# A hybrid attention layer: shift and scale rows of the second modulation summed on TensorE instead of VectorE

## The chip, the cores and the metric

The kernel runs on one core of a Trainium2 chip. A core has five engines that run side by side, each through its own list of instructions in order: TensorE (PE; its weight loads are shown apart as PEld), VectorE (DVE), ScalarE (ACT), GpSimd (POOL) and SyncE (SP), which here only starts transfers (DMAs). Matrix products go from the on-chip memory SBUF into the accumulator memory PSUM, from where DVE or ACT read them. The metric is the time of one execution on the device, in microseconds (us).

## What is computed

One layer of a streaming encoder on 1024 positions of width 1024, in float32. Cut to what the change concerns:

```python
mod = jnp.dot(jax.nn.silu(c), w_ada[l]) + b_ada[l]          # c: (1, 1024), w_ada: (1024, 6144)
sh_a, sc_a, g_a, sh_m, sc_m, g_m = jnp.split(mod, N_MOD, axis=-1)
h = modulate(rmsnorm(x, g_attn_norm[l]), sh_a, sc_a)        # h * (1 + scale) + shift
...
x = x + g_a[:, None, :] * mixed                             # attention groups, output projection
h = modulate(rmsnorm(x, g_mlp_norm[l]), sh_m, sc_m)
u = causal_dwconv(jnp.dot(h, w_up[l]), conv_w[l], conv_b[l])
gate, val = jnp.split(u, 2, axis=-1)
x = x + g_m[:, None, :] * jnp.dot(jax.nn.silu(gate) * val, w_down[l])
```

The six rows of `mod` are numbered 0 to 5. Row 2 is the gate of the mixer, row 3 the shift and row 4 the scale of the second modulation, the one ahead of the MLP. Each is a product of a vector of 1024 numbers with a 1024 x 1024 block of weights, which is 4 MB to read for one row of output.

## The kernel before

The kernel keeps nearly float32 accuracy in its large products by splitting operands into a high and a low part and adding three products (lines 154 to 156, one after another for each pair of tiles). It goes through these phases: the first modulation and the first query/key projection; attention, together with the remaining projections; the output projection; the MLP.

In the attention phase two kinds of work are woven together. *Units* are attention heads over four query tiles (`Unit.scores` makes scores on PE at L758, minimum on DVE at L775 to L783, exponential on ACT at L790, the two halves of the probabilities on POOL and DVE at L73 and L812, and their transposition by DMA at L824; `Unit.values`, three tiles behind, multiplies by the values on PE at L852 and writes through L861 and L862). *Fillers* are generators that do projections in small portions: v0, qk1, qk2, v1 (tiles `ipv`), qk3 (`ipq`), m (the latent projection, tiles `mp`), then up0, up1 and oca. After each part of a unit, `pace` runs as many portions of fillers as its own cost in PE time calls for. `gemm3_f` lets a portion follow the unit work of `LAG` steps ago (the list `trail`).

A third generator, `f_ada`, is the one that is changed. It computes rows 2, 3 and 4 on the side: `fill_step` calls it once for each 1700 ns of filler cost in the fillers qk1 to m. `steps` lists 48 blocks of weights: for each row m, each half n of 512 columns, each of the eight k of 128 input positions. A block is 128 partitions x 512 float32, 256 KB, loaded by SP (L409) into one of the five buffers with tag "A". Three blocks are loaded ahead. For each block DVE multiplies it by the column `cs[:, k]` of silu(c), which is one number to a partition, and adds it to an accumulator `aacc` of 128 x 512 (L421 for the first block, L423 for the rest). After eight blocks the accumulator still has to be summed over its 128 partitions. For row 2 `gate_bcast` does it with a product by a matrix of ones, which leaves the sum on all partitions. For rows 3 and 4 four products of PE, with 128 columns of the accumulator as the stationary operand and one column of ones as the moving one (L436), give the 512 sums as four columns of 128, in a PSUM buffer of tag "mm"; ACT copies them to `modT` (L437). `modT` rows 3 and 2 then get the bias, the 1 and the gain (L440 to L442), and are first read in the MLP's modulation.

The "mm" buffers are two; the projections of the fillers use them in turn.

The order of instructions on each engine isn't written out by hand: the units' parts have priorities, `issue_after` keeps an instruction behind another one, and a scheduler, which works with a model of the engines' times, places the rest. Each engine then takes its list strictly in that order.

Of the kernel before, what the change touches and what calls it, by code (L numbers as in the profile page):

```python
# [13 lines left out]
F32 = mybir.dt.float32  # L14
# [4 lines left out]
AF = mybir.ActivationFunctionType  # L19
# [3 lines left out]
MUL, ADD, SUB, MIN, MAX = ALU.mult, ALU.add, ALU.subtract, ALU.min, ALU.max  # L23

P = 128
D = 1024
S = 1024
NT = S // P
ND = D // P
# [9 lines left out]
GSTEP, LAG = 2, 4  # L39
# [25 lines left out]
def layer_kernel(ctx, tc, I, out):  # L65
    nc = tc.nc
    pe, act, dve, pool, sp = nc.tensor, nc.scalar, nc.vector, nc.gpsimd, nc.sync
# [22 lines left out]
    ga_d = dram.tile([P, D], F32, name="ga_d")  # L90
# [9 lines left out]
    ones = cst.tile([P, P], F32, name="ones")  # L100
# [3 lines left out]
    modT = cst.tile([P, 4, ND], F32, name="modT")  # L104
    cs = cst.tile([P, ND], F32, name="cs")
# [26 lines left out]
    ps = psA.__enter__()  # L132
# [6 lines left out]
    def qtile(name):  # L139
        return apg.tile([P, 512], F32, name=name, tag="sq", bufs=2)  # L140

    def atile(name):
        return apg.tile([P, 512], F32, name=name, tag="A", bufs=5)
# [17 lines left out]
    trail = []  # L161
# [115 lines left out]
    for d in range(ND):  # L277
# [7 lines left out]
        pt = ps.tile([P, 512], F32, name=f"p_ada{d}", tag="mm", bufs=2)  # L285
# [14 lines left out]
        for t in range(NT):  # L300
            h, j = divmod(t, 4)
# [97 lines left out]
    def f_ada():  # L399
        steps = [(m, n, k) for m in (2, 3, 4) for n in range(2) for k in range(ND)]  # L400
        wt = {}

        def load(i):
            if i < len(steps):
                m, n, k = steps[i]
                wt[i] = atile(f"aw{m}_{n}_{k}")
                c0 = m * D + n * 512
                with tc.issue_after(anchor["sp"]):
                    sp.dma_start(wt[i][:], I["w_ada"][k * P:(k + 1) * P, c0:c0 + 512])  # L409

        for i in range(3):
            load(i)
        yield 0
        yield 0
        for i, (m, n, k) in enumerate(steps):
            if k == 0:
                acc = atile(f"aacc{m}_{n}")
            load(i + 3)
            with tc.issue_after(anchor["dve"]):
                if k == 0:  # L420
                    dve.tensor_scalar(acc[:], wt[i][:], cs[:, 0:1], None, op0=MUL)  # L421
                else:
                    dve.scalar_tensor_tensor(acc[:], wt[i][:], cs[:, k:k + 1], acc[:], op0=MUL, op1=ADD)  # L423
            yield 0
            if k < ND - 1:
                continue
            yield 0
            pt = ps.tile([P, 512], F32, name=f"p_ada{m}_{n}", tag="mm", bufs=2)
            if m == 2:
                gate_bcast(pt[:], acc, m * D + n * 512, 512, qtile)  # L430
                g = qtile(f"gab{n}")
                act.activation(g[:], pt[:], AF.Copy)
                sp.dma_start(ga_d[:, n * 512:(n + 1) * 512], g[:])
            else:
                for j in range(4):
                    pe.matmul(pt[:, j:j + 1], acc[:, j * P:(j + 1) * P], ones[:, 0:1], start=True, stop=True)  # L436
                act.activation(modT[:, 3 if m == 3 else 2, 4 * n:4 * n + 4], pt[:, 0:4], AF.Copy)  # L437
            yield 0
        b = pk[:, C_B + 24:C_B + 40].rearrange("p (a b) -> p a b", a=2)
        dve.tensor_tensor(modT[:, 3, :], modT[:, 3, :], b[:, 0], op=ADD)  # L440
        dve.tensor_tensor(modT[:, 2, :], modT[:, 2, :], b[:, 1], op=ADD)
        dve.scalar_tensor_tensor(modT[:, 2, :], modT[:, 2, :], 1.0, pk[:, C_GM:C_GM + ND], op0=ADD, op1=MUL)  # L442

    def gate_bcast(pt, acc, c0, w, alloc):

        br = alloc(f"brow{c0}")
        sp.dma_start(br[0:1, :w], I["b_ada"][:, c0:c0 + w])
        dve.tensor_tensor(acc[0:1, :w], acc[0:1, :w], br[0:1, :w], op=ADD)
        pe.matmul(pt, ones[:], acc[:, :w], start=True, stop=True)
# [458 lines left out]
    def mla_unit(gr, hh, g):  # L908
        o = hh % 2

        def prep():
# [13 lines left out]
               ("m", f_m()), ("up0", f_up(0)), ("up1", f_up(1)), ("oca", f_oca())]  # L925
    done = set()
    side = [f_ada()]
    nside = [0]

# [47 lines left out]
    for n in range(len(tiles) + DEPTH):  # L977
        if n < len(tiles):
            u, i = tiles[n]
# [4 lines left out]
        if n >= DEPTH:  # L984
            u, i = tiles[n - DEPTH]
# [131 lines left out]
    for t in range(NT):  # L1117
        pt = ps2.tile([P, 1024], F32, name=f"op{t}", tag="op", bufs=3)
# [371 lines left out]
    for t in range(4):  # L1490
        o = dl.tile([P, 512], F32, name=f"oe{t}", tag="oe", bufs=3)
# [78 lines left out]
```

## Time and profile before

| | |
|---|---|
| median of 3 runs | 1380.44 us (1379.88 to 1385.12) |
| the profiled execution: time | 1379.88 us |
| the profiled execution: span, first to last instruction | 1378.1 us |
| mean granted TensorE clock | 0.94 |
| transfers of the 48 blocks `aw` | started between 114.1 and 325.5 us |
| rows 3 and 4: products at L436 | between 246.0 and 336.0 us |

The profile is of one execution. Busy times are of each engine alone, so they overlap. The end of a matmul is modelled, so that matmuls that follow each other closely show as a PE that is always busy; the distance between their starts is then the better measure. The granted clock (PEclk) is the share of full speed at which PE was let run. In the lists of waits, a row names the instruction that waited, what it waited for, the total in us, how many times, and the longest. In rows of a time line, the columns are the start in us, the length in us, engine, line, operation, what is written and read, and how many were merged into the row.

### The profile page before, as it was taken

To read this page: it belongs to the slowest core of one execution; us is meant where nothing else is said; L and a number is where in the kernel's file an instruction comes from. 1 tells how busy PE (TensorE), PEld (TensorE's weight loads), DVE (VectorE), ACT (ScalarE), POOL (GpSimd) and SP (SyncE) were. 2 spreads that over 40 slices of the span, in tenths; PEclk is the share of its full clock that TensorE was granted. 3 is DMA by queue.
4 is the path that set the end of the run, shared out by engine and by line. 5 is a ranking of instruction groups with operands and counts; after the bars stand their busy time and mean duration, and the time that the engine had idled before them with its cause. 6 is when DMAs were issued, how large, how long until landed. Compare 5 with 4: busy or idle time off the path is not lost.

```text
span 1378.1 us, 18696 instructions
## 1 busy us (share of the span) xinstructions
PE 1229.5 (89%) x6168; PEld 1009.3 (73%) x6168; DVE 1105.8 (80%) x1928; ACT 622.0 (45%) x1131; POOL 572.2 (42%) x610
## 2 busy tenths in 40 slices
PE   4889698989867779886997999999999999999998
PEld 3788487977655567674775888777788888888886
DVE  6957878676589997885689689898988888688667
ACT  4443445444455554554365443434444444443341
POOL 5454556365646574343643443434444442200000
PEclk9999797999787989997998999999999999999999
DMA  8314557666322468678921233333323224983451
GB/s 321 129 41 91 135 144 189 157 137 146 64 50 74 81 141 183 136 136 204 376 101 46 87 128 104 121 128 116 109 92 113 92 100 142 340 308 119 130 161 61
DMA packets 223689, 190.57 MB, mean 138 GB/s; under 512 B 148708, under 2 KB 166884, under 8 KB 223592
## 3 DMA queue, kind: packets, MB, share of 16 engines
q1 hardware_dynamic: 223592, 189.38, 47.5%
q8 instruction: 48, 0.79, 0.2%
q14 instruction: 49, 0.40, 0.1%
HBM read 117.24 MB, written 37.49 MB: 112 GB/s over the span
## 4 chain that ended last, share of the span: by engine, by line
PE 44%; DVE 16%; issue 5%; ACT 4%; DMA 4%; POOL 2%; SPq 0%; ACTq 0%; DVEq 0%; POOLq 0%
PE p L1068 6%; PE p L1070 6%; PE p L1069 6%; PE dnA_P L1381 2%; PE dnA_P L1383 2%; PE dnA_P L1382 2%; PE sm L764 2%; DVE u L1235 2%; PE dnB_P L1383 1%; PE dnB_P L1381 1%; PE dnB_P L1382 1%; DMA adaw<-w_ada 1%; DVE hlm L812 1%; DVE u L1234 1%; PE pvm L852 1%
## 5 line engine op out<-in xcount | busy, mean ns | idle before, releaser
L77 ACT ACTIVATE dnP<-dnr 128x1024 fp32r<-128x1024 f32 x73 | 77.4, 1062 | 113.1 <-PE dnA_P L1383 46.4
L1355 DVE TENSOR_TENSOR dnP<-dnr,dnP 128x1024 fp32r<-128x1024 f32 x72 | 89.5, 1246 | 46.5 <-ACT dnP L77 46.5
L73 POOL TENSOR_SCALAR hlm<-Pm,rim 128x512 f16<-128x512 f32 (+3 forms) x96 | 66.6, 702 | 75.8 <-ACT Pm L790 21.2
L1234 DVE SCALAR_TENSOR_TENSOR u<-c,cvp,u 128x1023 f32<-128x1023 f32 x44 | 62.0, 1449 | 29.6 <-ACT u L1233 29.6
L84 POOL TENSOR_TENSOR wf<-wu,wf 128x512 fp32r<-128x512 f32 x22 | 35.8, 1628 | 118.5 <-ACT wf L77 118.5
L73 POOL TENSOR_SCALAR hlc<-Pc,ric 128x640 f16<-128x640 f32 (+2 forms) x64 | 47.4, 744 | 72.2 <-DVE ric L793 40.6
L812 DVE SCALAR_TENSOR_TENSOR hlm<-Pm,rim,hlm 128x512 f16<-128x512 f32 (+3 forms) x96 | 67.7, 714 | 8.8 <-POOL hlm L73 8.4
L790 ACT ACTIVATE Pm<-sm,mm 128x128 f32<-128x128 f32 (+3 forms) x64 | 47.2, 738 | 52.5 <-DVE mm L783 31.8
L84 POOL TENSOR_TENSOR wb<-wu,wb 128x512 fp32r<-128x512 f32 x22 | 38.8, 1763 | 73.1 <-ACT wb L77 72.1
L1233 ACT ACTIVATE u<-c,cvp 128x1024 f32<-128x1024 f32 x44 | 52.3, 1237 | 34.4 <-DVE c L1304 25.8
L1235 DVE SCALAR_TENSOR_TENSOR u<-c,cvp,u 128x1022 f32<-128x1022 f32 x44 | 64.8, 1512 | 0.0
L852 PE MATMUL pvm<-PTm,vt 128*128 128x256 f16 (+1 forms) x320 | 45.9, 295 | 20.9 <-DMA PTm<-hlm 13.9
L790 ACT ACTIVATE Pc<-sc,mc 128x640 f32<-128x640 f32 (+2 forms) x64 | 42.0, 657 | 48.5 <-DVE mc L779 35.8
L812 DVE SCALAR_TENSOR_TENSOR hlc<-Pc,ric,hlc 128x640 f16<-128x640 f32 (+2 forms) x64 | 53.5, 840 | 12.7 <-POOL hlc L73 12.5
L852 PEld LDWEIGHTS <-vt 128*128 128x128 f16 x320 | 31.9, 109 | 35.7 <-DMA PTm<-hlm 14.4
L154 PE MATMUL ipq<-wq_s,hT 128*128 128x256 f32 x192 | 55.9, 294 | 1.2 <-ACT wq_s L77 1.2
L155 PE MATMUL ipq<-wq_s,hT 128*128 128x256 f32 x192 | 56.4, 294 | 0.1
L156 PE MATMUL ipq<-wq_s,hT 128*128 128x256 f32 x192 | 56.0, 292 | 0.0
L77 ACT ACTIVATE wc<-ws 128x512 fp32r<-128x512 f32 x21 | 13.3, 632 | 93.6 <-DVE ws L1087 93.6
L1382 PE MATMUL dnA_P<-dnP 128*128 128x512 f32 x132 | 51.3, 389 | 0.0
L1383 PE MATMUL dnA_P<-dnP 128*128 128x512 f32 x132 | 51.3, 389 | 0.0
L1381 PE MATMUL dnA_P<-dnP 128*128 128x512 f32 x132 | 51.2, 389 | 0.0
(432 smaller groups left out, 4453.4 us busy)
## 6 DMA issues: line engine op xcount, KB each, us to landing
wu<-w_up SPq DMA_DIRECT2D x44, 512.0 KB, 3.8
dnr<-g_d SPq DMA_DIRECT2D x73, 256.0 KB, 4.4
aw<-w_ada SPq DMA_DIRECT2D x48, 256.0 KB, 3.5
g_d<-u SPq DMA_DIRECT2D x22, 512.0 KB, 2.8
dnr<-w_down SPq DMA_DIRECT2D x44, 256.0 KB, 5.6
adaw<-w_ada_a SPq DMA_DIRECT2D x16, 512.0 KB, 6.1
x<-x SPq DMA_DIRECT2D x16, 512.0 KB, 9.0
g_d<-gs SPq DMA_DIRECT2D x22, 256.0 KB, 2.2
```

Source lines behind the costliest of these rows:

```text
L73: pool.tensor_scalar(o, i, s, 1.0, op0=MUL, op1=MUL)
L77: act.activation(o, i, AF.Copy)
L790: act.activation(pr[:, :n], sv, AF.Exp, bias=m[:], scale=-1.0, accum_out=rsum[:, 0:1])
L812: dve.scalar_tensor_tensor(hl[:, w:2 * w], pp, ri[:], hl[:, :w], op0=MUL, op1=SUB)
L852: last = pe.matmul(dst, u.vst(j), mov, start=(x == 0), stop=(x == len(todo) - 1), skip_group_check=True)
L1068: pe.matmul(pt, sh, pg[:, 0], start=(k == 0 and not add), stop=False, skip_group_check=skip)
L1069: pe.matmul(pt, sh, pg[:, 1], start=False, stop=False, skip_group_check=skip)
L1235: dve.scalar_tensor_tensor(u[:, 2:], c[:, :S - 2], cvp[:, cv:cv + 1], u[:, 2:], op0=MUL, op1=ADD)
L1355: r = f(*a, **k)
L1381: pe.matmul(pt, sh, w[:, 0, 0], start=start, stop=False, skip_group_check=add)
L1382: pe.matmul(pt, sh, w[:, 1, 0], start=False, stop=False, skip_group_check=add)
L1383: pe.matmul(pt, sl, w[:, 0, 0], start=False, stop=stop, skip_group_check=add)
```

## The change

Row 2 stays as it was. For rows 3 and 4, DVE no longer accumulates. Instead PE takes the weight blocks themselves as stationary operands, 128 x 128 at a time, with the column `cs[:, k]` as the moving operand, and sums over four blocks in PSUM: `burst` makes four products (q) for each of four column groups (j), 16 in all. Two bursts make one half of a row: ACT copies the first result to `modT`, DVE adds the second to it. There are eight bursts. The loads of these 32 blocks still go one to a step of the generator, through the same five buffers; a burst uses four of them, and is called five steps after its first block's load. The steps of row 2 no longer start loads for row 3. The generator takes 34 steps for rows 3 and 4 instead of 40.

```diff
+        def burst(i):
+            m, n, k0 = steps[i]
+            pt = ps.tile([P, 512], F32, name=f"p_ada{m}_{n}_{k0}", tag="mm", bufs=2)
+            for j in range(4):
+                for q in range(4):
+                    pe.matmul(pt[:, j:j + 1], wt[i + q][:, j * P:(j + 1) * P], cs[:, k0 + q:k0 + q + 1],
+                              start=(q == 0), stop=(q == 3))
+            o = modT[:, 3 if m == 3 else 2, 4 * n:4 * n + 4]
+            if k0:
+                dve.tensor_tensor(o, o, pt[:, 0:4], op=ADD)
+            else:
+                act.activation(o, pt[:, 0:4], AF.Copy)
+
...
-        for i, (m, n, k) in enumerate(steps):
+        nrow = 2 * ND
+        for i, (m, n, k) in enumerate(steps[:nrow]):
             if k == 0:
                 acc = atile(f"aacc{m}_{n}")
-            load(i + 3)
+            if i + 3 < nrow:
+                load(i + 3)
...
-            if m == 2:
-                gate_bcast(pt[:], acc, m * D + n * 512, 512, qtile)
-                g = qtile(f"gab{n}")
-                act.activation(g[:], pt[:], AF.Copy)
-                sp.dma_start(ga_d[:, n * 512:(n + 1) * 512], g[:])
-            else:
-                for j in range(4):
-                    pe.matmul(pt[:, j:j + 1], acc[:, j * P:(j + 1) * P], ones[:, 0:1], start=True, stop=True)
-                act.activation(modT[:, 3 if m == 3 else 2, 4 * n:4 * n + 4], pt[:, 0:4], AF.Copy)
+            gate_bcast(pt[:], acc, m * D + n * 512, 512, qtile)
+            g = qtile(f"gab{n}")
+            act.activation(g[:], pt[:], AF.Copy)
+            sp.dma_start(ga_d[:, n * 512:(n + 1) * 512], g[:])
+            yield 0
+        for i in range(nrow, len(steps) + 2):
+            if i % 4 == 1 and i > nrow + 1:
+                with tc.issue_after(trail[-1 - LAG]):
+                    burst(i - 5)
+            load(i)
             yield 0
```

## The prediction

> **What bounds the kernel now.** I read the page first (span, busy time, the chain that ended last), then the busy time by stage around the code that the change touches, then that code's own instructions in the same stages.
>
> ```profile
> span 1378.1 us, 18696 instructions
> PE 1229.5 (89%) x6168; PEld 1009.3 (73%) x6168; DVE 1105.8 (80%) x1928; ACT 622.0 (45%) x1131; POOL 572.2 (42%) x610
> PE 44%; DVE 16%; issue 5%; ACT 4%; DMA 4%; POOL 2%; SPq 0%; ACTq 0%; DVEq 0%; POOLq 0%
> ```
>
> PE (TensorE) is the busiest engine and has most of the chain. But a share over the whole span doesn't say what a local edit is worth; the edit lives between about 204 and 340 us:
>
> ```profile
> core 0: us, PE busy (x) PEld busy (x) DVE busy (x) ACT busy (x) POOL busy (x), PEclk, DMA share, GB/s
> 204.00:222.00 18.00, 12.67 (x55) 9.27 (x56) 16.44 (x40) 11.81 (x35) 12.17 (x14) 0.70 0.69 174
> 222.00:300.00 78.00, 78.00 (x556) 70.33 (x554) 57.13 (x155) 34.34 (x85) 44.56 (x55) 0.96 0.65 155
> 300.00:340.00 40.00, 34.91 (x188) 29.45 (x187) 29.65 (x80) 16.87 (x58) 26.26 (x52) 0.91 0.76 165
> 204.00:340.00 136.00, 125.59 (x795) 109.05 (x796) 103.22 (x274) 63.02 (x177) 83.00 (x119) 0.91 0.69 160
> ```
>
> In the middle 78 us PE is never idle and DVE (VectorE) has 21 us free. Only at the two ends does PE wait: 18.00 − 12.67 = 5.3 us, and 40.00 − 34.91 = 5.1 us, 10.4 in all. Who ends PE's waits, and what stands behind the largest of them:
>
> ```profile
> PE sc L758 <- ACT Pc L790: 3.6, 2, 1.9
> PE pvc L852 <- DVE oc L862: 2.2, 1, 2.2
> PE k_ps L692 <- DVE ql L717: 1.7, 1, 1.7
> PE pvc L852 <- DMA PTc<-hlc: 1.4, 1, 1.4
> PE mp L154 <- ACT modT L437: 0.9, 1, 0.9
> ...
> ACT Pc L790 <- DVE mc L779: 13.2, 5, 4.3
> ```
>
> The first three, 7.5 us, run through DVE (the softmax exponential L790 mostly waits for DVE's minimum, L779). So the ends are short of DVE and the middle is short of PE.
>
> **The change part by part.** *Removed from DVE:* the 32 accumulation steps for rows m = 3 and 4. The view by stage of the `aacc` instructions alone (PE, PEld, DVE):
>
> ```profile
> 204.00:222.00 18.00, 0.00 (x0) 0.00 (x0) 4.30 (x5) 0.70 0.69 174
> 222.00:300.00 78.00, 2.00 (x16) 1.95 (x16) 14.25 (x17) 0.96 0.65 155
> 300.00:340.00 40.00, 2.12 (x16) 2.00 (x16) 8.12 (x10) 0.91 0.76 165
> 204.00:340.00 136.00, 4.11 (x32) 3.94 (x32) 26.66 (x32) 0.91 0.69 160
> ```
>
> DVE loses 26.7 us, but 14.25 of them lie where PE never waited: there the time is hidden behind PE and worth nothing. In the two ends 12.4 us go, against 10.4 us of PE idle. The DVE-ended waits were 7.5 us, and between a quarter and a third of DVE's work there is aacc (4.30 of 16.44; 8.12 of 29.65), yet single steps stand straight ahead of what PE waits for. I give back half of 7.5: −3.7 us. Ends: 0 and −10.4.
>
> *Added to PE:* eight bursts of 16 products, 128 in place of 16. Each fp32 product leaves two records with a weight load of 128x128 each (16 gave x32 above), so 256 records for 32, 224 more. The old products have the same shape (128x128 fp32 stationary, one moving column), so their row is the price:
>
> ```profile
> 270.04 0.28 PE L155 MATMUL ipq<-wq_s,hT 128*128 128x256 f32 x1
> 270.16 0.28 PE L156 MATMUL ipq<-wq_s,hT 128*128 128x256 f32 x1
> 270.28 0.95 PE L436 MATMUL p_ada<-ones,aacc 128*128 128x1 f32 x8
> 271.09 0.36 PE L154 MATMUL ipq<-wq_s,hT 128*128 128x256 f32 x1
> ...
> 12.42 1.84 PE L288 MATMUL p_ada<-ones,adacc 128*128 128x1 f32 x8 [12.42 <-DVE adacc L273]
> ```
>
> 3.94 / 32 = 0.123 us each by the weight-load time, so 224 × 0.123 = +27.6 us, or 3.9 us a burst. Lower end, start to start in these rows: (271.09 − 270.28) / 8 = 0.101, +22.7 us. Upper end, by the matmul time 4.11 / 32 = 0.128: +28.8, and +3.4 more if one burst falls into a slow clock (1.84 / 8 = 0.23 in the last row, early in the run). A burst is as long as 32 projection matmuls (start to start 0.12 here), although it streams one column: the loads of consecutive products don't hide behind anything. Nothing else covers it, since PE takes its matmuls in order and the middle has no gap. By the built order six of the eight bursts fall among the v1 and qk3 projections, which is that middle, the last two among the latent projection; five are cut by score or value products of the attention units, which moves work but removes none.
>
> *The clock.* Part of the 10.4 us of waiting is paid twice, as the granted clock is low around it:
>
> ```profile
> 210.00:220.00 10.00, 6.58 (x28) 4.75 (x26) 9.65 (x22) 6.06 (x18) 8.47 (x8) 0.57 0.71 170
> 220.00:230.00 10.00, 10.00 (x47) 8.67 (x47) 8.91 (x26) 4.99 (x13) 7.72 (x10) 0.58 0.94 242
> 230.00:240.00 10.00, 10.00 (x79) 8.95 (x77) 7.76 (x31) 5.04 (x15) 6.10 (x8) 1.00 0.73 171
> ```
>
> 47 matmuls in a full 10 us at 0.58, 79 at 1.00. Busy time × (1 − clock) over the three stages is 12.67 × 0.30 + 78.00 × 0.04 + 34.91 × 0.09 = 3.8 + 3.1 + 3.1 = 10.0 us, the most that a full clock could return. If a good third of the idle goes, I take three tenths of it: −3.0 (ends 0 and −10.0). The Trainium skill (TensorE: Matmul & The Clock Gate, Part 1) says that the clock halves after an idle window of about 3.4 us and comes back after a busy one. These three rows agree in direction; by that rule, applied in full, the whole 10.0 would return, which is the first rival below.
>
> *New waits on PE.* A burst takes one of the two "mm" banks out of turn, eight times for four, and the next projection must wait until the bank is read. Of the four old groups one cost such a wait, 0.9 us (the `mp` row above). Four more groups at a quarter each: +0.9 us (ends 0 and 8 × 0.9 = 7.2). *Loads:* the count and the bytes stay, but four buffers now come free at once, when a burst ends, so four loads wait in SP's queue for PE, with projection weights and the transposes of later units behind them.
>
> ```profile
> 227.05 1.67 SPq L409 DMA_DIRECT2D aw<-w_ada  x3
> ...
> DMA to landing us min/median/max: 2.9/3.5/5.3
> ...
> DVE aacc L423 <- DMA aw<-w_ada: 3.7, 4, 1.8
> ```
>
> Four issues take 4 × 0.56 = 2.2 us and the last lands at most 5.3 later, 7.5 us after the burst. The shortest stretch between two bursts in the built order (second to third) has 42 projection matmuls (5.0 us) and 24 shorter ones or loads, some 7.7 us. The late transposes have units queued three deep ahead of them. So 0, but the margin is thin: a late load used to stop DVE (3.7 us), now it stops PE. *DVE's four new adds and ACT's four copies* are small, and off the path:
>
> ```profile
> L437 ACT ACTIVATE modT<-p_ada x4: 165/170/173, 247.1 to 337.0; 128x4 f32<-128x4 f32 x4
> L293 DVE TENSOR_TENSOR modT<-p_ada,pk x8: 143/148/150, 13.6 to 58.5; 128x1 f32<-128x1 f32 x8
> ```
>
> 4 × 0.15 = 0.6 us; their result is first used in the MLP, hundreds of us later. Hidden by that distance; uncovered it would be 0.6.
>
> *Sum* against the profiled execution (span 1378.1, its time 1379.88, which is 0.56 under the median 1380.44): 27.6 − 3.7 − 3.0 + 0.9 = **+21.8 us**, 1379.9 + 21.8 = 1401.7, or 1402 against the median.
>
> **The rivals.** *1. Relief pays in full.* All of PE's waits and the whole lost clock come back: 27.6 − 10.4 − 10.0 = +7.2, 1387. For it: DVE is over 90% busy at 204 to 222 and gates the exponentials. Against: one wait is a DMA's, and most DVE work there is not aacc.
>
> *2. Bursts wait for their weights.* The four loads share engines that are already 65 to 76% busy at 155 to 174 GB/s. At the stage's 160 GB/s one MB needs 6.6 us beside the rest; with 2.2 of issue and 3.5 to land that is 12 us, against stretches of 8 to 14. If each of seven stretches lost 2.4 us, +17: 21.8 + 17 = +39, 1419. For it: aw already came late four times with the loads spread out. Against: the lateness was 0.9 us a time.
>
> *3. Faster: the loads fit into gaps of the weight port.* PEld is busy 109.05 of 136, 27 us free, nearly the 27.6 that the bursts want. If PE's matmul time is only its modelled tail and weight loads decide, the bursts cost 27.6 − 27.0 = +0.6, and a full clock takes 10.0: −9.4, 1370.5. It decides from the point where a burst's records start well under 0.10 us apart in the stream. The Trainium skill (Perfetto Trace Analysis, Identifying the Most-Contended Engine) does say that matmul busy time is a bad measure of headroom and that LDWEIGHTS busy is the good one. By that rule there is room here. Against: loads of a burst follow each other and can't reach the gaps, which lie beside the 416 and 512 column products; the 0.101 row has the neighbours' overlap in it already.
>
> **How the numbers follow.** Forecast 0.57, first rival 0.16, second 0.17, third 0.10. Predicted is the forecast's 1402. The forecast's own bounds are 22.7 − 5 − 5 = +13 to 28.8 + 3.4 + 2 = +34. The range reaches below through most of the first rival, whose +7.2 has a spread of its own, and above to just short of the second: 1384 to 1417. Under 0.5% (6.9 us) can't be told from no change here. Slower: 0.57 + 0.17 and a third of the first rival, 0.79. Same: most of the rest of that rival and a little of the third, 0.12. Faster: 0.09.
>
> **What would show it.** Right: 256 records of one-column products with about 31 us of weight-load time; DVE some 26 us less; PE still without gaps through the projections, but for longer; the latent projection and all after it about 20 us late, and the span from there to the end as before. Wrong: a burst's pitch far from 0.123; PE waits of over 5 us named after `aw` (second rival); a clock near 1.00 where it was 0.57 (first); or a shift of more than 10 us that arises after 340 us, which none of these steps has, and which would come from the different order that the scheduler gives to later attention units.

## The result, and the profile after

| | before | after |
|---|---|---|
| median, runs of one comparison on one chip | 1380.99 us (4 runs, 1379.88 to 1385.12) | 1418.3 us (4 runs, 1416.37 to 1419.2) |
| ratio to before, with its 95% interval | | 1.0278 [1.0257, 1.0299] |
| profiled execution: time | 1379.88 us | 1416.37 us |
| profiled execution: span | 1378.1 us | 1414.6 us |
| mean granted TensorE clock | 0.94 | 0.925 |

The change makes the kernel 2.8% slower. The forecast was 1402 us with a range up to 1417, so the direction was right, and the time lies 16 us above the forecast and 1.3 us above the range. The same lines of the page, now of after:

```profile
span 1414.6 us, 19124 instructions
PE 1275.4 (90%) x6392; PEld 1052.2 (74%) x6392; DVE 1088.7 (77%) x1900; ACT 622.2 (44%) x1131; POOL 569.7 (40%) x610
PE 35%; DVE 9%; DMA 4%; issue 3%; POOL 1%; ACT 1%; SPq 1%; POOLq 0%; DVEq 0%; ACTq 0%
```

PE has 224 records more (6392 against 6168), as counted, but 45.9 us more busy time, where 27.6 were reckoned for them. So PE spends 18 us that no added instruction accounts for.

The busy time by stage around the bursts (columns: window, its length, then busy time and count of PE, PEld, DVE, ACT and POOL, the granted clock, DMA share, GB/s):

```profile
222.00:300.00 78.00, 78.00 (x506) 67.64 (x507) 49.73 (x152) 30.63 (x78) 32.73 (x43) 0.84 0.66 160
300.00:340.00 40.00, 40.00 (x295) 38.56 (x294) 5.57 (x10) 10.04 (x26) 15.76 (x25) 0.91 0.46 109
```

In the middle stage PE is busy all the time, before and after. But before it got 556 matmuls through 78 us at a clock of 0.96; now it gets 506 through, at 0.84. The clock fell in a stage where PE does not wait. The bursts alone, by the view of the `aw` instructions (PE, PEld, DVE), and PE's waits in the same stretch:

```profile
204.00:400.00 196.00, 31.59 (x256) 31.59 (x256) 0.00 (x0) 0.86 0.50 121
```

```profile
DVE modT L420 <- PE p_ada L416: 9.6, 3, 6.0
...
PE sc L774 <- ACT Pc L806: 2.8, 2, 1.9
...
PE sc L774 <- DVE k L739: 1.6, 1, 1.6
...
PE ipv L154 <- ACT wv_s L77: 1.2, 1, 1.2
```

31.59 / 256 = 0.123 us a record: by their own time the bursts cost just what the old products' row said. From start to start they are shorter. A burst at full clock that nothing interrupts:

```profile
259.91 3.63 PE L416 MATMUL p_ada<-cs,aw 128*128 128x1 f32 x32
263.40 0.36 PE L154 MATMUL ipv<-wv_s,hT 128*128 128x256 f32 x1
```

(263.40 − 259.91) / 32 = 0.109 us a record. Summed from the first record of each uninterrupted piece to the next other product, the 256 records take 29.5 us. No wait of PE names `aw`; the largest waits are 2.8 us and shorter. One wait is new: DVE's add of the second burst (L420) stood behind PE three times, 9.6 us in all, with all of DVE's work behind it. These adds start between 263.6 and 362.1 us, and from 232 to 366 us PE itself is never idle (shown below).

To see where the span grew, I cut both executions at the same events: the first product of filler qk1, the last product of the latent projection (m), the last product of the fillers up, the first product of the MLP (L1084 after), and the end. In the busy time by stage, before:

```profile
103.30:366.50 263.20, 234.56 (x1475) 200.07 (x1473) 195.25 (x540) 118.63 (x305) 144.90 (x208) 0.90 0.58 134
366.50:484.30 117.80, 85.60 (x404) 64.32 (x403) 101.11 (x298) 67.36 (x159) 67.82 (x78) 0.81 0.33 74
484.30:734.80 250.50, 214.47 (x1104) 169.46 (x1103) 200.54 (x405) 121.44 (x240) 115.03 (x129) 0.91 0.69 175
734.80:1378.10 643.30, 621.09 (x2693) 508.78 (x2691) 532.53 (x524) 268.52 (x343) 189.44 (x126) 0.98 0.39 134
```

and after:

```profile
107.40:399.00 291.60, 271.82 (x1698) 234.60 (x1697) 174.31 (x511) 119.39 (x305) 134.99 (x208) 0.87 0.51 121
399.00:513.00 114.00, 86.98 (x392) 67.09 (x391) 100.21 (x298) 66.18 (x158) 69.83 (x77) 0.78 0.37 76
513.00:775.30 262.30, 221.30 (x1116) 174.09 (x1115) 200.80 (x404) 122.28 (x241) 116.02 (x129) 0.89 0.67 167
775.30:1414.60 639.30, 620.07 (x2693) 508.66 (x2691) 535.90 (x527) 268.32 (x343) 194.27 (x126) 0.99 0.39 134
```

The span is 36.5 us longer. Of this, 107.4 − 103.3 = 4.1 arise before the first cut, where both kernels have the same instructions; 291.6 − 263.2 = **28.4 in the stretch with the bursts**; and −3.8, +11.8 and −4.0 in the three later stretches, +4.0 together. The 28.4 are 37.3 us more of PE's busy time (271.82 − 234.56) less 8.9 of idle time (28.6 to 19.8). Busy time × (1 − clock), summed over pieces of 2 us, gives the time lost to the clock: 22.1 us in this stretch before, 35.8 after, **+13.7**. The other 23.6 of the 37.3 are work, about what 224 more records cost at 0.109 us (24.4).

One burst seen closely shows how the clock goes. PE's time line of after, then the clock in steps of 2 us around it:

```profile
319.63 0.36 PE L156 MATMUL ipq<-wq_s,hT 128*128 128x256 f32 x1
319.84 4.21 PE L416 MATMUL p_ada<-cs,aw 128*128 128x1 f32 x32
323.90 0.56 PE L154 MATMUL ipq<-wq_s,hT 128*128 128x256 f32 x1
...
324.90 0.41 PE L155 MATMUL ipq<-wq_s,hT 128*128 128x256 f32 x1
325.12 0.41 PE L156 MATMUL ipq<-wq_s,hT 128*128 128x256 f32 x1
```

```profile
320.00:322.00 2.00, 2.00 (x21) 2.00 (x20) 1.01 (x3) 0.00 (x0) 0.32 (x2) 1.00 0.00 1
322.00:324.00 2.00, 2.00 (x15) 2.00 (x14) 0.00 (x0) 0.00 (x0) 1.92 (x2) 0.68 0.00 0
324.00:326.00 2.00, 2.00 (x11) 2.00 (x11) 0.16 (x1) 0.42 (x1) 2.00 (x4) 0.50 0.01 4
326.00:328.00 2.00, 2.00 (x11) 1.91 (x11) 0.00 (x0) 0.34 (x1) 0.82 (x2) 0.50 0.68 159
328.00:330.00 2.00, 2.00 (x14) 1.55 (x14) 0.00 (x0) 0.42 (x1) 0.92 (x2) 0.62 0.93 299
330.00:332.00 2.00, 2.00 (x12) 1.99 (x12) 0.00 (x0) 0.24 (x1) 0.00 (x0) 1.00 0.43 99
```

PE is busy in every one of these pieces, and its weight port nearly so. Yet from some 3 us into the burst until some 329 us the clock is at half, and the projection matmuls behind it start 0.22 us apart (324.90 to 325.12) where the prediction's rows showed 0.12. Three of the four old groups, of eight such records each, left the clock alone (before, around the group at 270.28):

```profile
270.00:272.00 2.00, 2.00 (x19) 2.00 (x18) 1.27 (x2) 1.11 (x2) 1.84 (x3) 1.00 0.54 139
272.00:274.00 2.00, 2.00 (x13) 1.44 (x11) 1.50 (x4) 1.36 (x4) 0.97 (x1) 1.00 0.14 33
```

Behind the fourth, at 312.34, the clock was at 0.50 from 314 to 316 us; but it had also been there from 308 to 310, and PE had been idle 0.24 us from 312 to 314, so that one does not tell.

It is not this burst alone. Seven of the eight bursts have such a fall in them or within 2 us behind them, and it lasts 3.4 or 6.8 us; only the fifth, from 307 to 311 us, has none. From 232 to 366 us, a time that holds all eight bursts, PE is never idle and the clock's mean is 0.89:

```profile
232.00:366.00 134.00, 134.00 (x891) 120.61 (x892) 59.01 (x181) 45.73 (x129) 55.50 (x97) 0.89 0.52 128
```

So theory 1 is that a burst's one-column products don't hold the clock up, and that the loss behind them is the part that the prediction lacked. The rivals: it is only the length of a burst that matters (shorter bursts cure it); the later units' order is the cause; or the loss comes from removing DVE's work and not from adding PE's.

### The profile page after: what moved, and what is told of

Its sections match the earlier page's. It is cut to its first block, busy times and chain, and to the rows that moved or that the text cites. A ratio compares the mean times of both kernels' runs of the same rounds, so it can differ in the third digit from the quotient of the medians.

```text
span 1414.6 us, 19124 instructions
## 1 busy us (share of the span) xinstructions
PE 1275.4 (90%) x6392; PEld 1052.2 (74%) x6392; DVE 1088.7 (77%) x1900; ACT 622.2 (44%) x1131; POOL 569.7 (40%) x610
## 4 chain that ended last, share of the span: by engine, by line
PE 35%; DVE 9%; DMA 4%; issue 3%; POOL 1%; ACT 1%; SPq 1%; POOLq 0%; DVEq 0%; ACTq 0%
PE p L1084 6%; PE p L1086 6%; PE p L1085 6%; PE dnA_P L1397 2%; PE dnA_P L1398 2%; PE dnA_P L1399 2%; DMA adaw<-w_ada 2%; DVE u L1251 2%; PE dnB_P L1399 1%; PE dnB_P L1398 1%; PE dnB_P L1397 1%; DVE u L1250 1%; ACT u L1249 1%; PE dnB L1399 1%; PE dnB L1398 1%
## 5 line engine op out<-in xcount | busy, mean ns | idle before, releaser
L73 POOL TENSOR_SCALAR hlm<-Pm,rim 128x512 f16<-128x512 f32 (+3 forms) x96 | 67.8, 715 | 92.4 <-DVE rim L809 28.3
L1249 ACT ACTIVATE u<-c,cvp 128x1024 f32<-128x1024 f32 x44 | 52.3, 1238 | 34.6 <-DVE c L1320 25.6
L154 PE MATMUL ipq<-wq_s,hT 128*128 128x256 f32 x192 | 58.4, 307 | 1.2 <-ACT wq_s L77 1.2
L155 PE MATMUL ipq<-wq_s,hT 128*128 128x256 f32 x192 | 58.6, 306 | 0.1
L156 PE MATMUL ipq<-wq_s,hT 128*128 128x256 f32 x192 | 58.4, 304 | 0.0
L868 PE MATMUL pvc<-PTc,v 128*128 128x256 f16 (+1 forms) x288 | 48.2, 299 | 3.7 <-DMA PTc<-hlc 3.6
L1398 PE MATMUL dnA_P<-dnP 128*128 128x512 f32 x132 | 51.4, 389 | 0.0
L1399 PE MATMUL dnA_P<-dnP 128*128 128x512 f32 x132 | 51.4, 389 | 0.0
```

What stands on the lines that cost most here:

```text
L73: pool.tensor_scalar(o, i, s, 1.0, op0=MUL, op1=MUL)
L868: last = pe.matmul(dst, u.vst(j), mov, start=(x == 0), stop=(x == len(todo) - 1), skip_group_check=True)
L1398: pe.matmul(pt, sh, w[:, 1, 0], start=False, stop=False, skip_group_check=add)
L1399: pe.matmul(pt, sl, w[:, 0, 0], start=False, stop=stop, skip_group_check=add)
```

## The experiments

The ratio is always to runs of the kernel before on the same chip, with its 95% interval. "Stretch" is the one from the first product of qk1 to the last of the latent projection, 263.2 us before and 291.6 after; "clock loss" is measured as above in that stretch.

**Sixty-four moving columns (wide64).** The same 128 products with the same weights, but the moving column is repeated 64 times; the first column of each group is read.

```diff
-                    pe.matmul(pt[:, j:j + 1], wt[i + q][:, j * P:(j + 1) * P], cs[:, k0 + q:k0 + q + 1],
-                              start=(q == 0), stop=(q == 3))
+                    pe.matmul(pt[:, j * P:j * P + 64], wt[i + q][:, j * P:(j + 1) * P],
+                              cs[:, k0 + q:k0 + q + 1].to_broadcast([P, 64]), start=(q == 0), stop=(q == 3))
...
+            r = pt[:].rearrange("p (a b) -> p a b", a=4)[:, :, 0]
...
```

> The same eight bursts, but with the moving column repeated to 64 columns (a broadcast read of cs; only the first result column of each group is used). The weight loads stay 256 and should still set the pace, about 0.12 us a record. Theory 1 (the granted clock falls to half after each burst because a product of one column counts as little activity): no fall of the clock after a burst, the part up to the last up projection 10 to 15 us shorter than in the changed kernel, about 1405 us in all. Rival A (the clock falls because of the weight loads themselves, or for a reason that has nothing to do with the bursts): clock and time as in the changed kernel, 1416 to 1420. Rival B (the extra time is made of waits for late blocks and banks): time as in the changed kernel, with the clock up.

Measured: 1405.29 us, 1.0177 [1.0156, 1.0199], 13.0 us under after by the medians. The products' own view, and the stretch with the pieces around one burst (which began at 253.56 and took 3.68 us):

```profile
204.00:400.00 196.00, 31.15 (x256) 30.26 (x256) 0.00 (x0) 0.92 0.57 130
```

```profile
106.20:386.10 279.90, 256.43 (x1698) 221.82 (x1697) 173.99 (x512) 119.33 (x305) 136.38 (x209) 0.92 0.55 126
...
254.00:256.00 2.00, 2.00 (x21) 2.00 (x19) 0.00 (x0) 0.00 (x0) 0.48 (x1) 1.00 0.42 75
256.00:258.00 2.00, 2.00 (x20) 1.85 (x19) 0.16 (x1) 0.00 (x0) 0.00 (x0) 1.00 0.46 121
258.00:260.00 2.00, 2.00 (x20) 1.84 (x19) 0.31 (x1) 0.80 (x2) 0.00 (x0) 1.00 0.92 308
```

The bursts cost the same (31.15 against 31.59 us) with 64 times the columns, so they are bound by their weight loads. The clock stays at 1.00 through and behind the burst shown, and so it does behind all eight, in the time that had 0.89 after:

```profile
232.00:361.00 129.00, 126.98 (x928) 115.87 (x928) 61.75 (x182) 46.97 (x129) 56.38 (x97) 1.00 0.60 140
```

The clock loss falls from 35.8 to 17.9 us and the stretch by 11.7. The order in which later units run also changed a little, as in every run here, so the 11.7 are not the clock's alone to a microsecond, but the place and the size fit. The weight loads are the same and the clock held, so it is not the loads themselves that let it fall. Theory 1 stands.

**Bursts of eight (burst8).** Sixteen bursts over two blocks each in place of eight over four.

```diff
-                for q in range(4):
+                for q in range(2):
...
-                              start=(q == 0), stop=(q == 3))
+                              start=(q == 0), stop=(q == 1))
...
-        for i in range(nrow, len(steps) + 2):
-            if i % 4 == 1 and i > nrow + 1:
+        for i in range(nrow, len(steps) + 4):
+            if i % 2 == 1 and i > nrow + 4:
```

> Sixteen bursts of eight products over two blocks, 1.95 us each, in place of eight of sixteen; the same 128 products, twelve DVE adds for four. Theory 1: a burst is shorter than the stretch of low activity that halves the clock, so fewer and shorter falls; about 1405 to 1410 us. Rival A: the same lost clock, about 1418. Rival B (waits for blocks and banks make the extra time): twice as many bank changes, so no shorter, 1418 or more.

Measured: 1415.67 us (1405.71 to 1418.71), 1.0229 [1.0184, 1.0273]; a wide spread, and not told apart from after. The clock loss is 32.8 us, 3.0 less. Its time line and its clock, around one short burst:

```profile
246.68 0.28 PE L156 MATMUL ipv<-wv_s,hT 128*128 128x256 f32 x1
246.80 1.84 PE L416 MATMUL p_ada<-cs,aw 128*128 128x1 f32 x16
248.50 0.36 PE L154 MATMUL ipv<-wv_s,hT 128*128 128x256 f32 x1
```

```profile
248.00:250.00 2.00, 2.00 (x14) 1.63 (x14) 1.53 (x7) 0.55 (x3) 1.46 (x3) 1.00 1.08 213
250.00:252.00 2.00, 2.00 (x6) 1.11 (x5) 1.31 (x5) 0.00 (x0) 0.09 (x1) 0.52 0.82 251
```

The clock falls some one and a half microseconds after a burst of only 1.84 us, with PE busy. Halving the bursts did not cure it, and the expectation that it would was wrong. But sixteen records don't always bring a fall. In the same run six other bursts of sixteen, starting 6 to 8 us apart, left the clock at 1.00:

```profile
294.50:338.00 43.50, 43.50 (x353) 42.63 (x352) 6.87 (x16) 12.11 (x29) 18.75 (x28) 1.00 0.54 128
```

At 338.15 two of them stood back to back, 32 records, and from 342.2 us the clock was at half again. What length or distance is enough wasn't found.

**Sixteen moving columns (wide16).** As wide64, with 16 in place of 64. Run once.

> The changed kernel with 16 moving columns. If what counts is the share of time in which columns stream, 16 columns are still little and the clock falls after the bursts as with one; about 1416 us. If any moving operand wider than one column suffices, about 1405.

Measured: 1423.36 us (one run, so no interval), clock loss 38.8 us. That is no better than one column. The time is of one run only, but its trace has the falls too, one with each of six of its eight bursts, and again PE is never idle around them:

```profile
232.00:366.00 134.00, 134.00 (x885) 121.09 (x884) 57.38 (x171) 45.11 (x128) 56.06 (x97) 0.87 0.52 124
```

Between 16 and 64 columns something changes that holds the clock up.

**The relief alone (relief).** No bursts and no sums: rows 3 and 4 of the modulation are left out and set to a constant; their 32 blocks are still loaded.

```diff
-            pt = ps.tile([P, 512], F32, name=f"p_ada{m}_{n}_{k0}", tag="mm", bufs=2)
...
-                act.activation(o, pt[:, 0:4], AF.Copy)
+            if not k0:
+                dve.memset(modT[:, 3 if m == 3 else 2, 4 * n:4 * n + 4], 0.01)
```

> The changed kernel with the bursts left out: rows 3 and 4 of the modulation are not summed (a constant stands in), the 32 blocks are still loaded. It shows what VectorE's 26.7 us are worth alone. The prediction gave them 3.7 us of waits and 3.0 of clock: about 1374 us. If all of PE's waits and the whole clock came back: about 1360. If the later units lose some 10 us in any order other than the one before: 1380 or more.

Measured: 1374.72 us, 0.9951 [0.9926, 0.9976]. The stretch:

```profile
104.30:360.70 256.40, 228.14 (x1443) 193.32 (x1442) 173.47 (x505) 118.59 (x301) 136.37 (x208) 0.91 0.59 137
```

It is 6.8 us shorter than before, near the 6.7 that the prediction gave to relief and clock together, but not by these parts. PE's idle time is 256.4 − 228.1 = 28.3 us, as good as unchanged from 28.6: with 21.8 us of DVE's work gone, PE waits as long as before. What went is PE's busy time, 6.4 us: about 4 for the sixteen old products that are missing here too (4.11 in the prediction's row), and some 3 of clock (22.1 to 18.7).

**The bursts alone (added).** Before, with DVE's accumulation in place, plus eight bursts of sixteen one-column products on one block, whose sums are not used.

```diff
+            if m > 2 and k % 4 == 3:
+                pt = ps.tile([P, 512], F32, name=f"p_adx{m}_{n}_{k}", tag="mm", bufs=2)
+                with tc.issue_after(trail[-1 - LAG]):
+                    for j in range(4):
+                        for q in range(4):
+                            pe.matmul(pt[:, j:j + 1], wt[i][:, j * P:(j + 1) * P],
+                                      cs[:, k:k + 1], start=(q == 0), stop=(q == 3))
+                    act.activation(cst.tile([P, 4], F32, name=f"adx{m}_{n}_{k}", tag="adx", bufs=2)[:], pt[:, 0:4],
+                                   AF.Copy)
```

> The kernel before with everything kept, and eight bursts of sixteen one-column products added beside it (each on one block, four times over; the sums are not used). It shows the price of the bursts alone. Prediction's price: 256 x 0.123 = 31.5 us, about 1412. Theory 1: 31.5 and some 15 us of halved clock, about 1427.

Measured: 1412.04 us, 1.0224 [1.0197, 1.0252].

```profile
104.10:400.20 296.10, 277.73 (x1730) 242.60 (x1729) 194.51 (x540) 120.05 (x313) 141.19 (x209) 0.86 0.51 120
```

By its time alone this run speaks for the prediction's price of a burst and against theory 1's, which was higher. By its parts it does not: the stretch is 32.9 us longer, made of 43.2 us more busy time of PE, with a clock loss of 39.7 (17.6 more than before), less 10.2 us of idle time (28.6 to 18.4). 43.2 less 17.6 is 25.6 us of work, 0.100 a record and not 0.123. Theory 1 had the clock's loss about right (some 15), took the work at 31.5, and had not reckoned that PE would wait less. And here DVE kept all of its work (194.51 against 195.25 us). So the shorter idle time that after shows too (8.9 us) appears without any relief of DVE. That a later PE waits less fits it, but is not shown apart from order, which moves the idle time by some 5 us in the runs with another order below.

**The bursts alone with 64 columns (added64).** As added, with the moving column repeated 64 times.

> The kernel before with the eight bursts added beside it, now with 64 moving columns instead of one. The kernel with one-column bursts added took 1412 us. If the low activity of one-column products costs its own part even with VectorE's work kept: 10 to 18 us less, 1394 to 1402. If not: 1408 to 1415.

Measured: 1403.27 us, 1.0165 [1.014, 1.0191]; the stretch:

```profile
107.30:389.60 282.30, 262.59 (x1730) 231.11 (x1729) 190.97 (x534) 119.15 (x311) 138.64 (x206) 0.91 0.53 124
```

8.8 us less than added, by the medians; the clock loss is 23.2 us in place of 39.7, the idle time 19.7. It was somewhat less than expected, but it is the second pair of kernels in which only the width of the moving operand differs, and in both the narrow one has the low clock and the longer stretch. In added six of the eight bursts bring a fall with PE not idle for 7 us ahead of it; in added64 there is no such fall.

**Another order alone (nudge1550, nudge1850).** After has 11.8 us more in the last stretch ahead of the MLP, that of the later units. To see what order alone does, these two are the kernel before with one number changed, how much filler cost there is between two steps of the generator; the instructions are the same. The diff is of the second; the first has 1550.

```diff
-                while nside[0] > 1700:
-                    nside[0] -= 1700
+                while nside[0] > 1850:
+                    nside[0] -= 1850
```

> The kernel before, with the side generator called for each 1550 ns of filler cost instead of 1700: the same instructions on every engine, in another order, as rows 2 to 4 are worked off some 10% earlier. Theory 2 (the changed kernel's extra microseconds after the projections, in the stretch of the output projection's first half, come from the other order of the later units and not from the bursts): that stretch (250 us before, 262 in the changed kernel) moves by 5 us or more here too, and the whole by some microseconds either way, 1373 to 1392. Rival (the bursts lengthen it): that stretch stays within 3 us of 250, the whole within 1377 to 1384.

> The same with 1850 ns, the rows worked off later. Theory 2: the stretch after the up projections moves by 5 us or more, the whole 1373 to 1392. Rival: stays within 3 us of 250, the whole 1377 to 1384.

Measured: 1382.39 us, 1.0007 [0.9981, 1.0032], with 1550, and 1374.17, 0.9949 [0.9932, 0.9965], with 1850. The stretch of the change and that of the later units, of 1550 and of 1850:

```profile
104.70:373.70 269.00, 238.60 (x1473) 201.12 (x1473) 195.76 (x540) 119.27 (x305) 145.97 (x209) 0.89 0.56 131
487.10:747.00 259.90, 219.45 (x1115) 173.33 (x1114) 197.27 (x402) 122.72 (x240) 112.52 (x128) 0.90 0.66 168
```

```profile
106.00:361.20 255.20, 231.76 (x1466) 198.69 (x1465) 196.41 (x536) 119.14 (x304) 142.41 (x208) 0.91 0.60 134
476.50:734.20 257.70, 219.01 (x1115) 172.97 (x1114) 199.51 (x405) 122.88 (x240) 118.67 (x128) 0.91 0.67 170
```

The later stretch grows by 9.4 and 7.2 us from order alone, to nearly what after shows (262.3), and part of it comes back in the MLP: from the last latent product to the end it is 1013.0 and 1011.7 us, against 1011.6 before and 1015.6 after. The other runs agree: that stretch is 252.3 us in wide64 and 252.7 in added, which have the bursts, and 259.4 in relief, which has none. So the late +11.8 needs no bursts to explain it, though how much of it is order alone stays open. But the stretch of the change moves by +5.8 and −8.0 too. Relief's −6.8 lies within what order does, and its parts above are worth no more than that. This also measures the noise of the other readings: by order alone the clock loss is 25.4 and 20.2 us (22.1 before) and PE's idle time 30.4 and 23.4 (28.6 before). The +13.7 of after and the +17.6 of added are far outside that; the differences of 3 us between clock losses are not.

The version with 1850 is the fastest of this study and beats both kernels: 0.5% under before, by order alone.

**The work where PE waits (defer_up, defer_up600, defer_up680, defer_all).** From wide64: rows 3 and 4 run beside the fillers up, where PE was idle for 117.8 − 85.6 = 32.2 us, one step for each 740, 600 or 680 ns of their cost; in defer_all beside up and oca, one for each 1850.

```diff
+        late[0] = True
...
-            if key not in ("v0", "up0", "up1", "oca"):
+            if key in ('up0', 'up1') if late[0] else key not in ("v0", "up0", "up1", "oca"):
...
-                while nside[0] > 1700:
-                    nside[0] -= 1700
+                while nside[0] > (740 if late[0] else 1700):
+                    nside[0] -= 740 if late[0] else 1700
                     next(side[0], None)
+                    if late[0] and key not in ('up0', 'up1'):
+                        break
```

> The kernel with 64 moving columns, with rows 3 and 4 taken out of the projections v1, qk3 and m, where PE has no gap, and run beside the fillers up0 and up1, where PE of the kernel before is idle 32 of 118 us (one step for each 740 ns of filler cost). If PE time in a full stage is what the bursts cost, the projections come about 7 us earlier than in the kernel before, as without the bursts, and up grows by less than the 31 us of the bursts: 5 to 20 us more; in all 1375 to 1395 us. If the bursts cost their 31 us wherever they stand: about 1405.

> The bursts beside up0 and up1 with 64 moving columns, one step for each 600 ns of filler cost instead of 740. The run at 740 had its projections and up 9 us shorter than the kernel before and gave back 15 in the stretch after. Theory 2: that stretch is drawn anew with each order; 1370 to 1395 us, faster than the kernel before if it comes out near 250. Rival (deferred bursts push the later units back): the stretch stays near 266, 1385 or more.

> The same with a step for each 680 ns. Theory 2: 1370 to 1395 us, by the stretch after the up projections. Rival: near 266 in that stretch, 1385 or more.

> As before, spread over up0, up1 and oca (one step for each 1850 ns of filler cost). PE of the kernel before is idle 68 of 368 us there. If idle time of PE takes the bursts, 1370 to 1390 us; if it can't, since those waits are for chains that the bursts lengthen, about 1405.

| | time, us | ratio to before | first stretch | up | later units | MLP |
|---|---|---|---|---|---|---|
| before | | | 263.2 | 117.8 | 250.5 | 643.3 |
| defer_up | 1387.82 | 1.0063 [1.004, 1.0086] | 253.7 | 118.7 | 266.0 | 638.0 |
| defer_up600 | 1380.0 | 0.9989 [0.9968, 1.0011] | 249.4 | 121.1 | 264.1 | 636.6 |
| defer_up680 | 1387.14 | 1.0053 [1.0026, 1.0081] | 253.7 | 125.4 | 253.6 | 644.5 |
| defer_all | 1401.24 | 1.0142 [1.0106, 1.0177] | 257.4 | 109.0 | 290.9 | 635.8 |

The stage up of defer_up, with all eight bursts in it:

```profile
360.70:479.40 118.70, 105.29 (x640) 90.74 (x640) 96.66 (x305) 62.38 (x154) 63.19 (x74) 0.87 0.57 141
```

236 records and 19.7 us of PE's busy time more than before, in a stage that became 0.9 us longer (3.3 and 7.6 with 600 and 680): where PE waits, the same bursts cost far less than their length. Yet none of these beat the kernel before by more than its measurement can tell. In defer_up and defer_up600 the later units take back 15.5 and 13.6 us. Whether that is order, as in the two kernels above, or something that the moved work does to these units, stays open; defer_up680, which has 253.6 there, loses the gain elsewhere. defer_all, whose last bursts fall among the later units, pays 40 us there and gets 8.8 in up and 7.5 in the MLP for it; it came out near its rival's 1405.

## Why the prediction was right in its sign and wrong in its size

*The bursts, +27.6: right in kind, some 3 to 4 too high.* The count and the records' own time came as reckoned: 256 records with 31.59 us, less the 3.94 of the old products, is 27.65. But a record's own time reaches over the start of the next product. Start to start it is 0.109 us at full clock, 24.4 us for 224, and the work in the stretch rose by 23.6. The prediction's lower end, 22.7, was taken start to start and was nearer.

***The clock,* −3.0: wrong, and the step that failed.** The prediction knew one reason for a low clock, waits of PE, and let the clock only gain from fewer of them; its ends, 0 and −10.0, held no loss. Measured: +13.7 us. The waits did become fewer, and relief's clock loss is about 3 us lower, the size that this term had in view, but no more than order alone does (+3.3 and −1.9). A stream of one-column products lets the clock fall by itself, with PE busy throughout. wide64 (17.9 us lost in place of 35.8) and added64 against added (23.2 and 39.7) show that it is the narrow products, and added shows that it needs no change on DVE. With the clock held, wide64 came to 1405.3, 3 us from the forecast, partly by luck: of the 24.3 us that its span is longer than before's, 16.7 lie in the stretch of the change and the rest ahead of it and behind it. The prediction had a slow burst as an upper end of the burst's own price, 3.4 us; it did not ask what a burst does to the matmuls behind it.

The Trainium skill (TensorE: Matmul & The Clock Gate, Part 1) lets the clock halve after an idle window of about 3.4 us. The time line of after doesn't agree if idle is read as a PE without instructions: the clock is 0.50 from 324 to 328 us, and in the pieces of 2 us around it PE is busy for 2.00 each. If the clock goes by how busy PE is, then 16 columns behind a 128x128 weight load don't count as enough and 64 do; what is counted, no run here shows.

*Relief of DVE and new waits, −3.7 + 0.9: a larger gain, and not by the reason given.* PE's idle time fell by 8.9 us and not by 2.8. That DVE's 26.7 us stand ahead of what PE waits for finds no support: relief took them away and left the idle time at 28.3, and added kept them and had 18.4. A term of 3.7 us is smaller than what order does to the idle time, though, so these runs can't exclude it. That a PE with more to do reaches its waits later fits all of them and is not shown. A wait of PE for a burst's bank to be read, the +0.9, does not show among its rows.

*Loads, 0, and DVE's adds, 0: right.* No wait of PE on `aw`, with the margin that was called thin. The adds brought waits of 9.6 us on DVE that weren't foreseen; they lay behind a PE without gaps.

*First rival, relief in full:* false; in relief PE's idle time did not go, and in after the clock fell. *Second rival, bursts that wait for weights:* its 1419 is the nearest number to the measured 1418.3, and its mechanism is absent. A time that fits shows nothing as long as the waits that it needs aren't in the trace. *Third rival, loads in the gaps of the weight port:* false. 27 us of that port were free, and the records of the bursts still took 29.5 us from start to start; what the Trainium skill (Perfetto Trace Analysis, Identifying the Most-Contended Engine) says of weight-load time as the measure of headroom didn't hold for them here, since a burst's loads follow one another.

*What would show it.* DVE's total fell by 17.1 us on the page, 20.9 in the stretch, and not 26. The latent projection ended 32.5 us later, of which 4.1 arose before the change. The shift of over 10 us after 340 us that was named as a sign of other order is there, 11.8, and the two kernels with another order show that order alone makes 7 to 9 of it and gives most of it back.

Together: +36.5 of span against +21.8 forecast. The clock is 16.7 of the difference, idle −6.1 and work −4.0 against it (the shorter pitch); the 4.1 ahead of the change and the 4.0 behind it make up the rest. The other kernels, which have the same instructions ahead of the change, come 0.8 to 4.6 us later than before there. The 4.0 behind it have no such explanation: from the last latent product to the end, the two kernels with another order differ from before by 1.4 and 0.1 us.

## What to carry to other kernels

A matmul with very few moving columns costs its weight load, and it can also cost the clock of everything that runs behind it; repeat the moving column to 64, which cost nothing here. Price an addition to PE in a stage where PE is never idle at its full length, start to start, and look for a stage where PE waits before making it cheaper. Where a scheduler places the work, run one or two kernels with the same instructions in another order before reading a difference under 1% as the worth of an edit.

## What was not expected of the hardware

- The granted clock falls to 0.50 some 3 us after the start of a stream of one-column fp32 products and stays there for some 7 us in the burst shown (322.7 to 329.5, from the clock of the 2 us pieces), with PE busy throughout. Sixteen columns don't prevent it (38.8 us lost in the stretch), 64 do (17.9).
- An fp32 product with 64 moving columns and 128x128 weights takes no longer than one with one: 31.15 against 31.59 us for 256 records.
- Sixteen one-column records, 1.84 us, can be followed by a fall (0.52 from one and a half microseconds later), but six bursts of sixteen in the same run were not (1.00 from 294.5 to 338 us); a group of eight, 0.95 us, left it at 1.00 in three of four places.
